# Gates, retention gate, retention queries and keys computed in one Strassen phase that leaves its results in DRAM

## The chip, the cores and the metric

The kernel runs on one core of one Trainium2 chip. The metric is the device time of one execution in microseconds (us). The median of three runs is taken; one further execution is recorded by the profiler.

## What is computed

One decoder block on x of 1024 rows and 1024 channels, all in float32. Cut to what matters here:

```python
xn = rmsnorm(x, norm1_g)
qa, ka, va, qr, kr, vr, gr, gate_a, gate_b = split(xn @ w_in)   # 3x1536, 1024, 1024, 2048, 2048, 1024, 1024 columns
# mixer A: 12 heads of 128 in three groups, dilated windows; the groups of a head slot are
# mixed by their softmax denominators
o_a = combine(attend(rmsnorm(qa), rmsnorm(ka), va))             # 1024 x 512
# mixer B: 4 retention heads, chunks of 128 rows, a state carried from chunk to chunk
o_r = head_groupnorm(retention(qr, kr, vr)) * silu(gr)          # 1024 x 2048
y = sigmoid(gate_a) * (o_a @ w_proj_a) + sigmoid(gate_b) * (o_r @ w_proj_b)
x = x + y @ w_out
x = x + square(relu(rmsnorm(x) @ w_up)) @ w_down
```

## The kernel before

**Arithmetic.** A float32 operand is kept as two tiles of the type fp32r, a rounded part (h) and the rest (l). `split` (L274 to L276) makes them: ScalarE copies h, VectorE subtracts to get l. Each product then takes three matmuls, h·h, h·l and l·h, which `Pipe.group` issues at L186. A *step* (`Pipe.step`, L195) is one such group for one PSUM tile, with small pieces of other work put between its matmuls: `pipe.at(lag, fn)` names a function that is to run inside the step that comes `lag` steps later. So the order on TensorE is written out by hand. The order on the other engines, and on SP's queue, from which every DMA is issued, is chosen by the framework's scheduler before the run, and each of these queues is worked off in that order.

**Weights.** `Weights` (L38) holds six pairs of buffers (wh, wl) of 1024 columns and three raw buffers, with a fourth (`more`) in the Strassen phase. A weight goes by DMA into a raw buffer (L140), and `split` takes it from there into a pair as soon as TensorE has freed that pair (`free`, L165). `add` queues one block; `add_units` (L88) queues a unit of the Strassen product, whose two raw blocks give four pieces, A, B and C of 1024 columns and D of 512, and on which VectorE makes four sums in place (`sums`, L111).

**Strassen.** A unit multiplies 256 weight columns with all 1024 rows and all 1024 channels. Directly that is 8 channel blocks x 4 PSUM tiles x 3 = 96 matmuls of 512 columns. The Strassen form takes 7 products of 4 blocks x 3 = 84 matmuls of 512 columns (`product`, L919, in `strassen_order`, L218). It needs seven tiles of operands: quarters of x and sums of them.

**Stages in order.** The norms and the attention, 12 heads of 8 steps (L410 to L516): each step projects queries, keys and values of one head for 128 rows (24 matmuls of 384 columns), and scores, turning and weighted values of earlier blocks run inside it. Then four retention heads (L564). Each projects its queries (`queries`, 4 steps of 24 matmuls of 512 columns) and its keys (8 steps of 24 matmuls of 256 columns, and `turn_k`, which turns each key block by two transposes). Then come 8 steps that project values, and inside these `decay` (scores of the chunk), `output`, `update` (the state) and `turn_o` run. `combine` (L529), which mixes the three attention groups, runs inside the value steps of the first three heads, for 128 rows at a time; it loads them by one DMA from `acc_d`. Then `gate` (L700) and `project` (L724): the gate projection `gr` for 256 columns, multiplied with the normalised retention output read back from `on_d`, and right behind it that slice's share of `o_r @ w_proj_b`, in groups of six matmuls, added up on VectorE in the SBUF tile `Y`. Then the merge (L781): both sigmoid gates, `o_a @ w_proj_a` (`merge`, L766), and the sum, split again into X. Then `w_out` with the second norm (L873), the up projection in Strassen form (L990) and the down projection (L1004).

Of the kernel before, what the change touches and what calls it, by code (L numbers as in the profile page):

```python
# [25 lines left out]
RH = 4  # L26
# [11 lines left out]
class Weights:  # L38
# [12 lines left out]
    def __init__(self, nc, rawp, wp, split):  # L51
# [6 lines left out]
        self.plain = self.taken = 0  # L58

# [10 lines left out]
    def add(self, src, buf=None):  # L70

        n = self.plain
        buf = n % self.WB if buf is None else buf
# [14 lines left out]
    def add_units(self, srcs):  # L88

        base = len(self.src)  # L90
        self.kept = {}
# [4 lines left out]
        def piece(key, buf, r, cols, then=None):  # L96
            def step():
                if isinstance(buf, tuple):
                    if "D" not in self.kept:
                        self.kept["D"] = self.buffer(buf[0])  # L100
                    h, l = (x[:, 512 * buf[1]:512 * buf[1] + 512] for x in self.kept["D"])
                else:
                    h, l = self.buffer(buf)
# [13 lines left out]
        for j in range(-1, len(srcs)):  # L117
            if j + 1 < len(srcs):
                r = base + 2 * (j + 1)
                piece((j + 1, "A"), self.A[(j + 1) % 2], r + 1, both)  # L120
            if j >= 0:
                r = base + 2 * j
                piece((j, "D"), (self.D, j % 2), r, slice(0, 512), lambda r=r: sums(r))
                piece((j, "B"), self.B[j % 2], r + 1, both, lambda r=r: self.used.add(r + 1))
                piece((j, "C"), self.C, r, both, lambda r=r: self.used.add(r))
# [18 lines left out]
    def pump(self, most=99):  # L144
        while most > 0 and self.next < len(self.steps):
# [3 lines left out]
            while len(self.raw) <= r:  # L149
                assert self.load()  # L150
# [80 lines left out]
def hybrid_block(ctx: ExitStack, tc: tile.TileContext, a: dict, out: bass.AP):  # L231
# [17 lines left out]
    oa_d = dram.tile([SLOTS, P, S], F, name="oa_d")  # L249
    on_d = dram.tile([NF, P, S], F, name="on_d")  # L250
    v_d = dram.tile([HEADS, S, DH], F, name="v_d")
# [39 lines left out]
    src = []  # L291
    for slot in range(SLOTS):
        for g in range(3):
            src += [a["w_att"][g * SLOTS + slot, u] for u in range(4)]
    for h in range(RH):
        src += [a["w_rqk"][h, u] for u in range(4)] + [a["w_rv"][h, u] for u in range(4)]
    src += [a["w_gr"][0, 0], a["w_gr"][0, 1]]
    for j in range(8):
        src += [a["w_pb"][j, 0], a["w_pb"][j, 1]]
        if j < 7:  # L300
            src += [a["w_gr"][j + 1, 0], a["w_gr"][j + 1, 1]]
    for d in range(KT):
        src += [a["w_gate"][d, 0], a["w_gate"][d, 1], a["w_pa"][d]]
    W = Weights(nc, rawp, wp, split)
    for ap in src:
        W.add(ap)
# [4 lines left out]
    W.add_units([a["w_up"][j] for j in range(NU)])  # L311
    for n, ap in enumerate([a["w_down"][c, nb, u] for c in range(8) for nb in range(2) for u in range(2)]):
# [801 lines left out]
```

## Time and profile before

| | |
|---|---|
| median of three runs | 2363.76 us (2363.75 to 2367.91) |
| the profiled execution: its own time | 2367.44 us |
| its span, first to last instruction | 2365.6 us |
| mean granted TensorE clock | 0.998 |
| instructions | 30143 |
| DMA traffic | 236.09 MB |

The page gives the busy time of each engine: PE is TensorE's matmuls, PEld its weight loads, DVE VectorE, ACT ScalarE, POOL GpSimd, and SP the queue that issues the DMAs. Matmuls overlap in their pipeline: a row that says that one took 390 ns does not say that the next began 390 ns later. The chain of work that ended last follows the execution back from its end, at each step to what released it; where it runs along TensorE for a while, its pieces give the true time from matmul to matmul. A view by stretches gives the busy time of each engine between two moments, the number of its instructions, the granted clock, and the share of time and the rate of the DMA engines.

### The profile page before, as it was taken

What the parts mean: (1) busy time and instruction counts of PE and PEld (TensorE: products, weight loads), DVE (VectorE), ACT (ScalarE), POOL (GpSimd) and SP (SyncE); (2) the same over time, 40 slices, a digit from 0 to 9 for tenths busy, and PEclk for the clock granted to TensorE, in tenths of its full rate; (3) what the DMA queues carried; (4) which work ended last, traced back from release to release, by engine and by line L of the source; (5) the groups of instructions that cost most, each with busy time, mean ns of one, the idle gap of its engine ahead of it and who ended that gap; (6) DMA issues with size and microseconds to landing.
All of it is one profiled execution on the core that took longest, in us unless ns stands there. A gap on an engine that the chain in (4) does not pass through costs nothing.

```text
span 2365.6 us, 30143 instructions
## 1 busy us (share of the span) xinstructions
PE 2337.6 (99%) x11704; PEld 2017.1 (85%) x11704; DVE 1112.2 (47%) x2316; ACT 832.0 (35%) x1904; POOL 101.3 (4%) x148
## 2 busy tenths in 40 slices
PE   8999999999999999999999999999899999999999
PEld 7999999998788888878888888888788888788887
DVE  6344443444837353654555542243855555133532
ACT  6444444443424333442211221132566656210010
POOL 1111111110000000000000000000000000000000
PEclk9999999999999999999999999999999999999999
DMA  4212122132321211132222221115244447733601
GB/s 138 81 54 88 57 57 87 52 108 70 106 81 59 71 50 50 54 99 63 78 74 63 72 76 49 45 46 176 90 162 167 160 166 265 286 132 113 248 27 72
DMA packets 118049, 236.09 MB, mean 100 GB/s; under 512 B 8721, under 2 KB 53905, under 8 KB 113810
## 3 DMA queue, kind: packets, MB, share of 16 engines
q1 hardware_dynamic: 117906, 234.17, 30.2%
q8 instruction: 92, 1.51, 0.3%
q14 instruction: 51, 0.42, 0.1%
HBM read 171.12 MB, written 63.01 MB: 99 GB/s over the span
## 4 chain that ended last, share of the span: by engine, by line
PE 92%; DVE 4%; ACT 1%; issue 1%; DMA 1%; POOL 1%; SPq 0%; POOLq 0%; ACTq 0%; DVEq 0%
PE mm L186 68%; PE ms L186 18%; PE ms L451 1%; PE ms L431 1%; PE tr L497 1%; PE ms L444 1%; DVE xl L276 1%; PE tr L673 1%; PE ms L619 0%; DVE St L664 0%; POOL st L649 0%; DVE Sl L276 0%; ACT xh L275 0%; PE tr L598 0%; DVE wl L276 0%
## 5 line engine op out<-in xcount | busy, mean ns | idle before, releaser
L186 PE MATMUL mm<-wh,xh 128*128 128x384 f32 (+2 forms) x1792 | 677.6, 378 | 3.5 <-ACT Yd L1015 3.5
L186 PE MATMUL mm<-wh,xl 128*128 128x384 f32 (+2 forms) x1792 | 632.2, 353 | 2.4 <-DVE xl L276 2.3
L186 PE MATMUL mm<-wl,xh 128*128 128x384 f32 (+2 forms) x1600 | 556.8, 348 | 0.9 <-DVE wl L276 0.9
L276 DVE TENSOR_TENSOR wl<-raw,wh 128x1024 fp32r<-128x1024 f32 (+2 forms) x240 | 265.7, 1116 | 252.9 <-ACT wh L275 251.1
L186 PEld LDWEIGHTS mm<-wh,xh 128*128 128x128 f32 x1792 | 338.9, 189 | 34.4 <-ACT Yd L1015 3.9
L275 ACT ACTIVATE wh<-raw 128x1024 fp32r<-128x1024 f32 (+2 forms) x240 | 231.2, 971 | 388.3 <-PE mm L186 268.0
L186 PEld LDWEIGHTS mm<-wh,xl 128*128 128x128 f32 x1792 | 338.2, 189 | 34.4 <-DVE xl L276 3.7
L186 PE MATMUL mm<-xh,wh 128*128 128x512 f32 x896 | 352.3, 393 | 0.0
L186 PE MATMUL mm<-xl,wh 128*128 128x512 f32 x896 | 349.5, 390 | 1.7 <-DVE xl L276 1.7
L186 PE MATMUL mm<-xh,wl 128*128 128x512 f32 x896 | 349.4, 390 | 0.0
L186 PEld LDWEIGHTS mm<-wl,xh 128*128 128x128 f32 x1600 | 303.7, 190 | 23.2 <-DVE wl L276 1.6
L186 PEld LDWEIGHTS mm<-xl,wh 128*128 128x128 f32 x896 | 168.7, 188 | 36.1 <-DVE xl L276 2.1
L186 PEld LDWEIGHTS mm<-xh,wl 128*128 128x128 f32 x896 | 168.6, 188 | 35.5
L186 PEld LDWEIGHTS mm<-xh,wh 128*128 128x128 f32 x896 | 168.7, 188 | 34.5
L1017 DVE TENSOR_TENSOR Yd<-Yd,mm 128x512 f32<-128x512 f32 x112 | 76.9, 686 | 172.3 <-PE mm L186 171.6
L186 PE MATMUL ms<-oh,wl 128*128 128x512 f32 x256 | 101.1, 395 | 0.0
L186 PE MATMUL ms<-oh,wh 128*128 128x512 f32 x256 | 101.1, 395 | 0.0
L186 PE MATMUL ms<-ol,wh 128*128 128x512 f32 x256 | 101.0, 395 | 0.0
L438 ACT ACTIVATE pr<-s,acc 128x128 f32<-128x128 f32 (+1 forms) x96 | 43.1, 449 | 149.3 <-DVE acc L436 132.2
L733 DVE TENSOR_TENSOR Y<-Y,ms 128x512 f32<-128x512 f32 x112 | 76.1, 685 | 38.1 <-PE ms L186 37.5
L285 POOL TENSOR_TENSOR ssa<-ssa,half 128x2 f32<-128x2 f32 x96 | 66.2, 690 | 423.0 <-DVE ssa L284 418.6
L186 PE MATMUL mm<-wh,h 128*128 128x512 f32 x256 | 79.1, 389 | 0.0
(187 smaller groups left out, 2951.8 us busy)
## 6 DMA issues: line engine op xcount, KB each, us to landing
h_d<-hs SPq DMA_DIRECT2D x64, 512.0 KB, 4.0
raw<-in_w_att SPq DMA_DIRECT2D x48, 384.0 KB, 3.9
raw<-in_w_up SPq DMA_DIRECT2D x32, 512.0 KB, 3.8
raw<-in_w_down SPq DMA_DIRECT2D x32, 512.0 KB, 4.5
xh<-h_d SPq DMA_DIRECT2D x12, 1024.0 KB, 7.2
xl<-h_d SPq DMA_DIRECT2D x12, 1024.0 KB, 8.1
raw<-in_w_rqk SPq DMA_DIRECT2D x16, 512.0 KB, 4.5
raw<-in_w_rv SPq DMA_DIRECT2D x16, 512.0 KB, 3.9
```

Of the source, the lines that this page charges most:

```text
L186: self.nc.tensor.matmul(ps, x, y, start=start, stop=stop, skip_group_check=not first)
L275: nc.scalar.activation(dst_h, src, AF.Copy)
L276: nc.vector.tensor_tensor(dst_l, src, dst_h.bitcast(F), op=OP.subtract)
L285: nc.gpsimd.tensor_tensor(dst, dst, half[:, :w], op=OP.pow)
L431: nc.tensor.matmul(sp[:, :n], qT[:, b * P:(b + 1) * P], kT[:, k0:k0 + n], start=True, stop=True)
L438: nc.scalar.activation(st["p"][:, :n], s[:, :n], AF.Exp, bias=acc[:, b, DH:DH + 1], accum_out=acc[:, b, DH + 1:DH + 2])
L444: nc.tensor.transpose(tp[:, j * P:(j + 1) * P], st["p"][:, j * P:(j + 1) * P], ident)
L451: nc.tensor.matmul(po[:, :DH], st["t"][:, j * P:(j + 1) * P], V[:, k0 // P + j, :], start=(j == 0), stop=(j == nk - 1))
L497: nc.tensor.transpose(pt[:, j, :], qk[:, j, :], ident)
L673: nc.tensor.transpose(pt[:, f, :], it["o"][:, f * P:(f + 1) * P], ident)
L733: nc.vector.tensor_tensor(Y[:, d, cs], Y[:, d, cs], pp, op=OP.add)
L1017: nc.vector.tensor_tensor(Y[:, t, ns], Y[:, t, ns], pm, op=OP.add)
```

## The change

- The order of the heads in the last slot becomes 1, 2, 0, so that the group without dilation comes last. `combine` takes 512 rows of one slot instead of 128 rows of four, with four DMAs instead of one. Six of its eight calls move into the attention steps, two stay in the first retention head.
- Behind the attention a new phase computes, from X, all of gate_a, gate_b, qr, kr and gr. The first three of eight gate pairs are computed directly (12 steps of 24 matmuls), while the memory of the attention comes free and `differences` builds the four further Strassen operands. Then 21 Strassen units run: 5 gate pairs, 8 of queries and keys, 8 of gr. Their results go by DMA to `sg_d` (through a sigmoid), `rqk_d` and `sr_d` (times its sigmoid).
- Retention projects values only. `load_chunk` reads queries and keys of a chunk back, two chunks ahead; `decay` turns the keys by two transposes before it scales them. `load_oa` splits the mixed attention output in the last four chunks.
- Then `o_a @ w_proj_a` runs for all channels, 16 steps of 12 matmuls; each result is multiplied with its gate, read back from `sg_d`, and stored in `pa_d`. Beside these steps `load_o` reads `on_d` and `sr_d`, and makes and splits the operand of the retention projection, 16 row tiles in halves of 512 columns. That projection then runs in two chunks of 8 row tiles, 16 steps of 24 matmuls each: the first leaves its results in `pb_d`, the second adds them, gate and attention part, and splits the sum into X.
- `product` becomes a function for both Strassen phases, with its text otherwise unchanged; the buffers behind a Strassen phase follow the order in which its pieces come free (`cycle`). `Y` is gone.

The core of the diff:

```diff
+    heads = [(slot, g) for slot in range(SLOTS) for g in ((0, 1, 2) if slot < SLOTS - 1 else (1, 2, 0))]
+    W.add_units("in", [a["w_gate_q"][j] for j in range(NG)] + [a["w_rqk_q"][j] for j in range(NQ)]
+                + [a["w_gr_q"][j] for j in range(8)])
...
+    def combine(s, i, p2b):
+        at = p2b.tile([P, 4, 3, DH + 2], F, name="at", bufs=1)
+        rows = acc_d[512 * i:512 * i + 512].rearrange("(t p) (g s) e -> s p t g e", p=P, s=SLOTS)
+        for t in range(4):
+            nc.sync.dma_start(at[:, t], rows[s, :, t])
...
+                if head in (5, 8, 11) and b in (1, 5):
+                    pipe.at(2, combine((head - 5) // 3, b // 5, cmb))
...
+    def gate_out(f, d, cs, src):
+        sg = sgp.tile([P, 512], F, name="sg")
+        nc.scalar.activation(sg, src, AF.Sigmoid)
+        nc.sync.dma_start(sg_d[f, d, :, cs], sg)
...
+                    def differences(k):
+                        x = {}
+                        for j, i in ((0, 0), (0, 1), (1, 1), (1, 0)):
+                            x[j, i] = xp.tile([P, 512], F, name=f"x{j}{i}")
+                            xh, xl = XS[j, i]
+                            nc.vector.tensor_tensor(x[j, i], xh[:, k].bitcast(F), xl[:, k].bitcast(F), op=OP.add)
+                        for name, t, u, op in (("N5", (0, 0), (0, 1), OP.subtract), ("N7", (0, 1), (1, 1), OP.subtract),
+                                               ("N6", (1, 1), (0, 0), OP.add), ("N4", (1, 0), (1, 1), OP.subtract)):
+                            nc.vector.tensor_tensor(x[t], x[t], x[u], op=op)
+                            split(operands[name][0][:, k], operands[name][1][:, k], x[t])
...
+        def result(j, f, cs, src):
+            if j < NG:
+                gate_out(f, 3 + j, cs, src)
+                return
+            n = j - NG
+            sg = src
+            if n >= NQ:
+                sg = sgp.tile([P, 512], F, name="sg")
+                nc.scalar.activation(sg, src, AF.Sigmoid)
+                nc.vector.tensor_tensor(sg, src, sg, op=OP.mult)
+            elif src.space == PSUM:
+                sg = sgp.tile([P, 512], F, name="sg")
+                nc.scalar.activation(sg, src, AF.Copy)
+            nc.sync.dma_start(sr_d[2 * (n - NQ) + f, :, cs] if n >= NQ else rqk_d[n // 2, n % 2, f, :, cs], sg)
+        for j, name in strassen_order(NG + NQ + 8):
+            product("in", j, name, unit, operands, lambda: pu, result)
...
+            qk = [p2.tile([P, 2, P], F, name=x, bufs=3) for x in ("rqT", "rkT")]
+            for i in range(2):
+                nc.sync.dma_start(qk[i], rqk_d[h, i, :, :, ts].rearrange("f p t -> p f t"))
...
                     if c < NT - 1:
+                        pt = tr.tile([P, 4, P], F, name="tr")
+                        for f in range(2):
+                            nc.tensor.transpose(pt[:, f, :], kT[:, f], ident)
...
+                if h == 0 and c in (1, 4):
+                    pipe.at(2, combine(SLOTS - 1, c // 4, p2b))
+                if h == RH - 1 and c >= 4:
+                    load_oa(c - 4)
...
+        pm2 = pool(ph, "pm2", 2)
+        def load_o(places, n):
+            for place in places:
+                for cs in halves():
+                    o, sr = loaded(on_d[n, :, cs], "s1"), loaded(sr_d[n, :, cs], "s2")
+                    nc.scalar.activation(o, o, AF.Identity, scale=gng[:, 0, n:n + 1], bias=gng[:, 1, n:n + 1])
+                    nc.vector.tensor_tensor(o, o, sr, op=OP.mult)
+                    split(place[:, 0, cs], place[:, 1, cs], o)
+                n += 1
+        load_o(oS, 0)
+        for d in range(KT):
+            ua, = W.take(1)
+            uh, ul = W[ua]
+            for cs in halves():
+                sga = loaded(sg_d[0, d, :, cs], "s0")
                 pp = ms.tile([P, 512], F, name="ms")
+                pipe.step(pp, [(uh[:, k * P:(k + 1) * P], ul[:, k * P:(k + 1) * P], oaS[k][0][:, cs], oaS[k][1][:, cs])
+                               for k in range(SLOTS)], {SLOTS - 1: lambda: W.free(ua)} if cs.start else None)
+                nc.vector.tensor_tensor(sga, sga, pp, op=OP.mult)
+                nc.sync.dma_start(pa_d[d, :, cs], sga)
+                if ES is None and not pipe.due:
                     ret.close()
+                    ext = pool(body, "ext", 3, "right")
+                    ES = [slot_of(ext) for _ in range(3)] + [slot_of(pool(e1, "ext1", 1, "right"))]
+                    load_o(as_rows(ES[0]) + as_rows(ES[1]), 4)
+                    load_o(as_rows(ES[2]) + as_rows(ES[3]), 12)
+        load_o(places, 8)
...
         for d in range(KT):
+            ub, = W.take(1)
+            for cs in halves():
+                pp = project(0, d, cs, ub)
+                t = pm2.tile([P, 512], F, name="s0")
+                nc.scalar.activation(t, pp, AF.Copy)
+                nc.sync.dma_start(pb_d[d, :, cs], t)
...
+        for n, (d, cs) in enumerate(work):
+            if n + 1 < len(work):
+                ahead.append(fetch(n + 1))
+            y, sgb, pa = ahead[n]
+            pp = project(1, d, cs, ub)
+            nc.vector.tensor_tensor(y, y, pp, op=OP.add)
+            nc.vector.tensor_tensor(y, y, sgb, op=OP.mult)
+            nc.vector.tensor_tensor(y, y, pa, op=OP.add)
+            split(*X(d, cs), y)
```

`as_rows` views the two tiles of an operand slot as two places of 2 x 1024 columns (h and l); `fetch(n)` loads `pb_d`, `sg_d` and `pa_d` of one step; `project(c, d, cs, ub)` is one step of 24 matmuls over the eight places of chunk c.

More of the change, by code (lines that the diff above doesn't have):

```diff
@@ L408, in hybrid_block @@
         nc.sync.dma_start(dist, a["c_dist"])
-        for head in range(HEADS):
-            slot, g = divmod(head, 3)
+        for head, (slot, g) in enumerate(heads):
             h = g * SLOTS + slot
@@ new lines, in hybrid_block @@
+        ahead = [fetch(0)]
+        for n, (d, cs) in enumerate(work):
+            if cs.start == 0:
+                ub, = W.take(1)
+            if n + 1 < len(work):
[6 more added lines that the diff above has]
+            split(*X(d, cs), y)
+        e1.close()
@@ L1073, in r @@
         return np.arange(lo, lo + n)
+    gates = [np.concatenate([r(GA + d * P, P), r(GB + d * P, P)]) for d in range(KT)]
     a = {
```

498 lines of the change are left out of this document (225 added, 273 removed).

## The prediction

> **What bounds the kernel now.** I read the page first, part 1 and then part 4, the chain of work that ended last.
>
> ```profile
> PE 2337.6 (99%) x11704; PEld 2017.1 (85%) x11704; DVE 1112.2 (47%) x2316; ACT 832.0 (35%) x1904; POOL 101.3 (4%) x148
> PE 92%; DVE 4%; ACT 1%; issue 1%; DMA 1%; POOL 1%; SPq 0%; POOLq 0%; ACTq 0%; DVEq 0%
> ```
>
> TensorE is busy 99% of the span and 92% of the chain lies on it. So a matmul that disappears is worth its own time, if its stage keeps TensorE fed. How much is that? A page row for a 512-column matmul says about 390 ns, but these overlap. Two pieces of the chain in order of time give the true distance:
>
> ```profile
> 1048.99 11.19 PE ms L186 x48
> 1060.18 10.89 PE mm L186 x48
> ```
>
> 10.89 / 48 = 0.2269 us in a projection of long groups; 11.19 / 48 = 0.233 us in `project`, with its groups of six. Last, the view by stretches: the attention; the last retention head whole; its value steps alone; gate, project and merge together; the restart in the second norm; the up projection, which is already in Strassen form; and the 10 us with the densest DMA in packets of 2 KB.
>
> ```profile
> core 0: us, PE busy (x) PEld busy (x) DVE busy (x) ACT busy (x) POOL busy (x), PEclk, DMA share, GB/s
> 10.50:517.80 507.30, 504.47 (x3102) 492.70 (x3101) 221.66 (x720) 233.62 (x904) 69.86 (x102) 1.00 0.24 73
> 902.60:1027.00 124.40, 124.40 (x678) 107.44 (x677) 58.66 (x125) 44.66 (x81) 6.43 (x8) 1.00 0.19 55
> 949.20:1027.00 77.80, 77.80 (x372) 64.72 (x371) 48.18 (x103) 33.30 (x60) 5.88 (x7) 1.00 0.22 68
> 1027.00:1598.00 571.00, 569.34 (x2491) 466.93 (x2490) 257.71 (x362) 131.79 (x187) 0.55 (x1) 1.00 0.21 66
> 1692.80:1715.00 22.20, 15.69 (x66) 12.31 (x67) 19.99 (x33) 11.12 (x18) 0.55 (x1) 0.85 0.19 60
> 1715.00:2010.80 295.80, 295.80 (x1307) 244.91 (x1306) 163.67 (x216) 184.25 (x298) 0.00 (x0) 1.00 0.53 184
> 2000.00:2010.00 10.00, 10.00 (x46) 8.27 (x45) 3.28 (x4) 5.27 (x8) 0.00 (x0) 1.00 1.01 336
> ```
>
> Everywhere around the change TensorE is busy all the time, and no other engine is over two thirds full.
>
> **The gross gain, from matmul counts.** Queries and keys: a head takes 124.40 us, its value steps 77.80, so 46.60 us go into them, 186.4 us for four heads. In Strassen form they are 8 units x 84 matmuls x 0.2269 = 152.5 us. The keys must still be turned, now inside `decay`: 4 heads x 7 chunks x 2 = 56 transposes. Four transposes in a row take from 1035.42 to the next matmul at 1035.80, 0.095 us each:
>
> ```profile
> 1035.42 0.63 PE L673 MATMUL tr<-ident,on 128*128 128x128 f32 x4 [1.66 <-DVE on L651]
> 1035.80 0.48 PE L186 MATMUL mm<-xh,wh 128*128 128x512 f32 x1
> ```
>
> That is 5.3 us. Gain: 186.4 - 152.5 - 5.3 = **28.6 us**.
>
> The stretch of 571.0 us holds 768 matmuls of gr, 768 of the retention projection, 768 of the gates and 192 of the attention projection, 2496. After the change they are 8 x 84 = 672, 768 in long groups, 3 x 96 + 5 x 84 = 708, and 192: 2340 x 0.2269 = 531.0 us. Gain: **40.0 us**, of which 156 matmuls make 35.4; the rest is the shorter distance in long groups and the wait of 1.66 us above, for which I charge anew below. Gross: 68.6 us.
>
> The attention's own work only moves: the last group trails by fewer steps, but every score is still computed. `w_out`, up and down keep their counts.
>
> **Does the Strassen phase keep TensorE fed?** A unit lasts 84 x 0.2269 = 19.06 us. The prices of its work beside TensorE:
>
> ```profile
> L276 DVE TENSOR_TENSOR wl<-raw,wh 128x1024 fp32r<-128x1024 f32 x168 | 203.9, 1223 | 241.0 <-ACT wh L275 239.8
> L275 ACT ACTIVATE wh<-raw 128x1024 fp32r<-128x1024 f32 x168 | 175.7, 1057 | 359.0 <-PE mm L186 259.3 <-PE ms L186 73.2 <-DMA raw<-in_w_up 16.1
> L720 DVE TENSOR_TENSOR sg<-sg,oi 128x512 f32<-128x512 f32 x32 | 22.1, 691 | 0.9
> L717 ACT ACTIVATE sg<-mm 128x512 f32<-128x512 f32 x32 | 19.0, 594 | 129.2 <-PE mm L186 129.1
> ```
>
> VectorE: 3.5 splits x 1.22, four sums, two subtractions and, for gr, four products of 0.69: 11.2 us of 19.06, 59%. ScalarE: 3.5 x 1.06 + 7 x 0.59 = 7.8 us, 41%. The up projection ran beside 55% and 62% with TensorE busy 295.80 of 295.80 us, so I charge nothing here. DMA: about 1 MB in and 1 MB out per 19 us is 110 GB/s, against 184 in the up projection. The cover is thinner only at the start: `differences` costs VectorE 4 x 12 x 0.69 = 33 us, which has to fit between the attention's tail and the first N6. From the fifth of the twelve direct gate steps on, these leave 7 x 24 x 0.2269 = 38 us, and four products of 2.7 us follow before N6: 49 us, against 33 plus some 10 us of weight pieces. I charge 1 us, between 0 and 5.
>
> One price there is new, since sigmoids of the gates and exponentials of the attention's tail now alternate on ScalarE. Before, there was one change of function table within the program:
>
> ```profile
> 1029.03 1.28 ACT L717 ACT_TABLE_LOAD   x1
> 1030.40 0.60 ACT L717 ACTIVATE sg<-mm 128x512 f32<-128x512 f32 x1
> ```
>
> From the load to the next activation it took 1.37 us. I count five changes in the first three gate steps, 6.9 us, beside ScalarE's own 233.62 / 96 = 2.4 us per attention step, 7.3 us for three: 14 of 16.3 us, so it fits, and I charge 0, at most 2. [...]
>
> **`combine` in the attention.** VectorE works 221.66 of 507.30 us there, so there is room for six bursts of some 5.5 us. The stall that it can make is that of an engine held by a load. So far, eight calls cost TensorE less than this row, which also holds the 1.66 us at the end of retention:
>
> ```profile
> PE tr L673 <- DVE on L651: 4.6, 6, 1.7
> L535 DVE TENSOR_TENSOR w<-at 128x4 f32<-128x4 f32 x8 | 1.3, 160 | 9.3 <-DMA at<-acc_d 9.3
> ```
>
> VectorE stood 9.3 us in eight calls. With four DMAs and short lags I take 2 us more, between 0 and 12 (six times a burst's 5.5 us less the slack, 2 us a call).
>
> **The tail of retention.** Behind the last `output` came 24-matmul steps; now there are steps of 12, 2.72 us. The chain to `turn_o` took this long:
>
> ```profile
> 1028.42 0.60 ACT L644 ACTIVATE on<-ms 128x512 f32<-128x512 f32 x1 [2.90 <-PE ms L186]
> 1032.87 0.55 DVE L719 TENSOR_SCALAR oi<-oi,gng 128x512 f32<-128x512 f32 x1 [3.13 <-DMA oi<-on_d]
> 1033.33 0.18 DVE L647 BATCH_NORM_AGGREGATE st<-st 128x2 f32<-128x6 f32 x1
> ```
>
> 1028.42 to 1035.42 is 7.0 us, 3.13 of them VectorE standing before a load. Without that it is 3.9 against a cover of 12 matmuls, 2.72: at least 1 us late; with a load of `load_o` in front, 4.3. I take 3.
>
> **The attention projection with `load_o` beside it: the main cost.** TensorE needs 192 x 0.2269 = 43.6 us, with the last output group 45.6. Behind it stands the first step over chunk 0, which needs eight row tiles, 16 halves. The prices:
>
> ```profile
> oi<-on_d SPq DMA_DIRECT2D x32, 256.0 KB, 2.7
> y_d<-xr SPq DMA_DIRECT2D x16, 256.0 KB, 2.1
> xh<-h_d SPq DMA_DIRECT2D x12, 1024.0 KB, 7.2
> h<-h_d SPq DMA_DIRECT2D x8, 1024.0 KB, 12.6
> ```
>
> - A half: load 2.7, then 0.59 + 0.69 + 0.59 + 0.69; 5.3 us, two buffers, so one per 2.6 us: 16 take 42 us.
> - A step's gate: load 2.7, product 0.69, store 2.1, two buffers: 2.75 us per step, against 2.72 on TensorE.
> - VectorE: 32 + 16 operations of 0.69 and some 6 us of weight splits: 39 us.
> - DMA: 14 halves x 0.52 MB, 14 gates and 15 stores x 0.26, 2.1 MB of weights: 17.0 MB. At the 336 GB/s of the full queue above (share 1.01): 51 us.
>
> So four limits lie between 39 and 51 us where TensorE wants 45.6. Nothing is free to catch up, `load_o` of the later tiles competes, and a load that is late holds VectorE for all. A gain is excluded, since TensorE's matmuls remain. Bounds: 0, and 30 (below). The nearest row is the full queue, 51; I add 8 us for queueing: **13 us**.
>
> Afterwards there is cover again: 24 matmuls, 5.45 us, over three loads (0.79 MB, with weights 190 GB/s) and 3.4 us of VectorE.
>
> **Sum.** 68.6 - 1 - 2 - 3 - 13 = 49.6 us. The profiled execution took 2367.44 us (span 2365.6), 3.7 above the median of 2363.76. So 2317.8 against its own time, and **2314 us** against the median.
>
> **Rivals.**
>
> A: the projection is not held up; DMA and VectorE run ahead, as each limit alone nearly allows. Then 68.6 - 6 = 62.6: 2301 us. For it: three of four limits are below TensorE's.
>
> B: the queue is paced by loaded latency. The same 1 MB load takes 7.2 us or 12.6 where DMA is full, 1.75 times. A gate round is then (4.7 + 0.7 + 3.7) / 2 = 4.55 us, 16 make 73 us, and with queueing TensorE loses 30. Short waits also cost clock: the stretch from 1692.80 got 0.85 of it, 3.3 us lost in 22.20, though its longest wait is this:
>
> ```profile
> PE tr L834 <- DVE x L854: 2.9, 1, 2.9
> ```
>
> Total 68.6 - 6 - 30 - 3 = 29.6: 2334 us. [...]
>
> C: the Strassen phase does not deliver, because 21 units with more results than pairs of buffers run 2 us late each: 42 us lost, net 8, 2356 us. Against it: the up projection's 295.80 of 295.80.
>
> D, slower: SP works its queue in order, and in the attention a weight load can wait long.
>
> ```profile
> SPq L140 <- DVE wl L276: 885.4, 142, 34.8
> SPq L531 <- DVE oa L551: 12.7, 4, 8.9
> ```
>
> If the four loads of `combine` stand behind such a wait of up to 34.8 us, VectorE stands with them, and TensorE after two steps, 2 x 5.28 us: over 20 us six times. 49.6 - 120 = -70: 2434 us. It decides from 49.6 / 6 = 8.3 us per call. Against it: so far these loads waited only for their own buffer, 12.7 us in four times.
>
> **Chances.** Forecast 0.53, A 0.20, B 0.15, C 0.05, D 0.07. About 0.2% (4.7 us) can be told from no change. C lies partly within that: 0.03 same, 0.02 faster. Faster 0.90, same 0.03, slower 0.07. The range takes in the forecast with its bounds, A and B: A with the unknown costs at 0 is 2295, B with the end of `combine`'s range at 12 is 2344; C and D, 0.12, are left out. So 2293 to 2344.
>
> **What would show it.** Right: in the Strassen phase 19.1 us per unit and TensorE without gaps; value steps of 79 us per head; between the last value step and the first step over chunk 0 some 58 us, with waits for VectorE and loads and a DMA share near 1. Wrong: waits there under 5 us (A) or over 25 (B); waits of TensorE in the attention behind `combine`'s loads (D); N-products that wait for weights or `differences`; more than ten table loads.

## The result and the profile after

The changed kernel takes 2365.48 us (median of 20 runs, 2362.87 to 2370.16), the kernel before 2365.11 us in the same session: a ratio of 1.0003, with an interval of 0.9996 to 1.001. No change can be measured, although TensorE has 644 of its 11704 matmuls and transposes less to do. The profiled execution took 2367.1 us, its span is 2365.3. Its page, parts 1 and 2:

```profile
PE 2292.8 (97%) x11060; PEld 1961.2 (83%) x11060; DVE 1169.9 (49%) x2372; ACT 926.5 (39%) x2030; POOL 102.0 (4%) x148
...
PE   8999999999999999999999869999899999999999
...
PEclk9999999999999999999999979999999999999999
```

TensorE is busy 45 us less in a span of the same length, and a dip, in TensorE's row and in that of the clock, lies around slices 23 and 24, that is from 1300 to 1420 us. The view by stretches, cut at the first matmul of each stage, has the same columns as before:

```profile
10.50:537.50 527.00, 513.85 (x3140) 499.16 (x3139) 250.37 (x895) 238.76 (x932) 70.17 (x102) 0.99 0.28 84
537.50:611.00 73.50, 72.56 (x339) 58.94 (x338) 48.31 (x92) 34.69 (x65) 0.69 (x1) 1.00 0.27 95
611.00:1014.00 403.00, 400.64 (x1766) 331.06 (x1765) 186.39 (x232) 149.67 (x216) 0.00 (x0) 1.00 0.36 114
1014.00:1332.40 318.40, 313.08 (x1505) 257.19 (x1505) 205.17 (x489) 140.58 (x259) 24.36 (x31) 0.99 0.30 86
1332.40:1429.20 96.80, 61.81 (x211) 47.53 (x210) 51.26 (x78) 42.87 (x61) 0.55 (x1) 0.79 0.82 264
1429.20:1603.20 174.00, 174.00 (x769) 144.10 (x768) 73.19 (x96) 45.70 (x63) 0.00 (x0) 1.00 0.53 170
1603.20:2365.00 761.80, 751.29 (x3329) 620.60 (x3327) 350.43 (x483) 269.40 (x428) 5.52 (x8) 1.00 0.46 159
```

They are the attention, the direct gate steps, the Strassen phase, the value steps, the attention projection, the retention projection, and all that is from `w_out` on. Beside the terms of the forecast (its sum of 49.6 us, from a span of 2365.6, is a span of 2316.0):

| stage | forecast, us | measured, us | difference |
|---|---|---|---|
| attention, to the last matmul of 384 columns | 517.8 + 2 | 536.7 | +16.9 |
| direct gate steps | 75.5 (what the sum leaves) | 74.4 | -1.1 |
| Strassen phase | 21 x 19.06 + 1 | 402.9 | +1.6 |
| value steps | 4 x 79 | 318.3 | +2.3 |
| attention projection, with retention's tail | 45.6 + 13 + 3 | 96.8 | +35.2 |
| retention projection | 768 x 0.2269 | 174.1 | -0.2 |
| from `w_out` to the end | 767.5 | 762.1 | -5.4 |

The differences add up to the missing 49.3 us. Two stages hold it. In the attention projection TensorE stands still for 35.0 us; and it is busy 61.8 us with matmuls that need 45.6 at full clock, 16.2 us more. Most of that is the clock, 0.79 on average: it stood at half for 41.0 us of the stage, and TensorE worked in 28.4 of these. Its matmuls came 0.427 us apart there, against 0.228 at full clock. By the granted share that costs 14.2 us, by the distances 13.2, both estimates. What TensorE waited for, in the whole kernel (engine and line, what released it: us in total, times, longest):

```profile
PE ms L193 <- DVE s L856: 28.4, 5, 8.8
...
PE ms L193 <- ACT smh L287: 3.6, 1, 3.6
...
PE tr L800 <- DVE on L779: 3.1, 1, 3.1
PE ms L549 <- DVE pT L544: 3.1, 4, 1.4
PE mm L193 <- ACT wh L287: 3.1, 2, 2.8
```

The first is the attention projection: L856 is the product of a result with its gate, which frees the PSUM tile. The second is the first retention step, whose mask landed late. The third is the tail of retention. The last two, with parts of others, are the attention. The stretch of the attention projection in the view of waits, all engines:

```profile
ACT s L836 <- DMA s<-on_d: 31.3, 18, 3.4
PE ms L193 <- DVE s L856: 28.4, 5, 8.8
...
DVE s L837 <- ACT s L836: 23.4, 14, 2.8
...
DVE s L856 <- DMA s<-sg_d: 3.8, 4, 1.8
```

ScalarE stands before `load_o`'s loads, VectorE behind ScalarE, TensorE behind VectorE. The gate's own load is hardly waited for, 3.8 us. What holds the gate's product (L856) is its place: in VectorE's fixed order 22 of `load_o`'s products (L837), one for each half, stand before the thirteenth gate's. That one frees the PSUM tile of the sixteenth and last step, since there are three such tiles. The first and the sixteenth of these products:

```profile
1341.45 0.69 DVE L837 TENSOR_TENSOR s<-s,s 128x512 f32<-128x512 f32 x1 [1.38 <-DMA s<-sr_d]
...
1396.41 0.69 DVE L837 TENSOR_TENSOR s<-s,s 128x512 f32<-128x512 f32 x1 [1.15 <-ACT s L836]
```

So the halves come 54.96 / 15 = 3.66 us apart. The first comes 9.1 us into the stage and the twenty-second 88.2 us; right behind it, at 88.8 and 90.2 us, come the products of the twelfth and the thirteenth gate. The DMA of the stage:

```profile
DMA packets 13619, 25.55 MB, mean 264 GB/s; under 512 B 1423, under 2 KB 2447, under 8 KB 13614
...
s<-on_d SPq DMA_DIRECT2D x25, 256.0 KB, 3.6
s<-sr_d SPq DMA_DIRECT2D x25, 256.0 KB, 3.5
raw<-in_w_pb SPq DMA_DIRECT2D x8, 512.0 KB, 5.5
s<-sg_d SPq DMA_DIRECT2D x15, 256.0 KB, 4.0
pa_d<-s SPq DMA_DIRECT2D x13, 256.0 KB, 3.9
```

25 halves are read there, of which the next stage needs 16 at its start, and eight weight blocks, with which it begins one by one.

In the attention, the loss sits at three changes of head. At the first, after head 4, VectorE and then ScalarE (start, duration, and in brackets the idle time before, with what ended it):

```profile
227.24 0.17 DVE L405 TENSOR_TENSOR w<-at 128x4 f32<-128x4 f32 x1 [3.76 <-DMA at<-acc_d]
...
229.71 0.95 DVE L288 TENSOR_TENSOR wl<-raw,wh 128x768 fp32r<-128x768 f32 x1
```

```profile
227.99 0.21 ACT L409 ACTIVATE w<-w 128x12 f32<-128x12 f32 x1 [4.82 <-DVE w L408]
228.11 1.56 ACT L287 ACTIVATE wh<-raw 128x768 fp32r<-128x768 f32 x2
```

```profile
228.99 0.45 PE L193 MATMUL mm<-wh,xh 128*128 128x384 f32 x1 [0.31 <-ACT wh L287]
230.72 0.52 PE L193 MATMUL mm<-wl,xh 128*128 128x384 f32 x1 [1.28 <-DVE wl L288]
```

This is the second call of `combine` for its slot. Its loads were issued at 221.88, as soon as the first call had read its buffer for the last time, and the scheduler put its first operations at the end of the head. There both engines stand in order before its loads, and right behind in both queues wait the weight pieces of the next head, for which TensorE stands. The second change of head goes the same way, with waits of 2.8 and 1.3 us. At the third, after head 10, VectorE stands before these loads too (3.2 and 2.3 us), but TensorE then waits for pieces of the attention itself (`pT` and `pr`), 4.3 us in five waits. After each of the first two the granted clock was half for 3.4 us, and TensorE's matmuls came 0.32 us apart in place of 0.173; the waits before the first were of 0.3 and 1.3 us.

### The profile page after: what moved, and what is told of

Read it like the earlier page. It is cut to its first block, busy times and chain, and to the rows that moved or that the text cites. A ratio compares the mean times of both kernels' runs of the same rounds, so it can differ in the third digit from the quotient of the medians.

```text
span 2365.3 us, 29821 instructions
## 1 busy us (share of the span) xinstructions
PE 2292.8 (97%) x11060; PEld 1961.2 (83%) x11060; DVE 1169.9 (49%) x2372; ACT 926.5 (39%) x2030; POOL 102.0 (4%) x148
## 4 chain that ended last, share of the span: by engine, by line
PE 45%; DVE 2%; DMA 1%; ACT 1%; issue 1%; POOL 0%; SPq 0%; POOLq 0%; ACTq 0%; DVEq 0%
PE mm L193 35%; PE ms L193 9%; DMA s<-on_d 1%; DVE xl L288 0%; ACT xh L287 0%; PE tr L800 0%; PE ms L744 0%; DMA s<-sr_d 0%; DVE xn L988 0%; ACT s L836 0%; DVE s L837 0%; POOL ssq L297 0%; ACT wh L287 0%; ACT mm L981 0%; DMA s<-sg_d 0%
## 5 line engine op out<-in xcount | busy, mean ns | idle before, releaser
L193 PE MATMUL mm<-wh,xh 128*128 128x384 f32 (+1 forms) x1536 | 604.2, 393 | 3.1 <-ACT wh L287 3.1
L193 PE MATMUL mm<-wh,xl 128*128 128x384 f32 (+1 forms) x1536 | 561.2, 365 | 2.0 <-DVE xl L288 1.9
L193 PE MATMUL mm<-wl,xh 128*128 128x384 f32 (+1 forms) x1344 | 485.9, 362 | 2.6 <-DVE wl L288 2.6
L193 PE MATMUL mm<-xh,wl 128*128 128x512 f32 x720 | 281.0, 390 | 0.0
L193 PE MATMUL ms<-xh,wh 128*128 128x512 f32 x604 | 244.2, 404 | 34.2 <-DVE s L856 28.4
L193 PE MATMUL ms<-xl,wh 128*128 128x512 f32 x604 | 240.8, 399 | 0.0
L193 PE MATMUL ms<-xh,wl 128*128 128x512 f32 x604 | 239.9, 397 | 0.0
L193 PEld LDWEIGHTS ms<-xh,wh 128*128 128x128 f32 x604 | 116.9, 194 | 61.8 <-DVE s L856 24.9
L193 PEld LDWEIGHTS ms<-xh,wl 128*128 128x128 f32 x604 | 116.7, 193 | 25.0
L193 PEld LDWEIGHTS ms<-xl,wh 128*128 128x128 f32 x604 | 116.7, 193 | 23.6 <-DVE xl L288 0.3
L536 ACT ACTIVATE pr<-s,acc 128x128 f32<-128x128 f32 (+1 forms) x96 | 43.2, 450 | 148.9 <-DVE acc L534 135.5
```

The source lines that it names most:

```text
L193: self.nc.tensor.matmul(ps, x, y, start=start, stop=stop, skip_group_check=not first)
L536: nc.scalar.activation(st["p"][:, :n], s[:, :n], AF.Exp, bias=acc[:, b, DH:DH + 1], accum_out=acc[:, b, DH + 1:DH + 2])
```

## The experiments

The theories that the runs were to tell apart: **H**, the engines that stand before `combine`'s loads with the next head's weights behind them cost the 17 us. For the attention projection: **B**, its length is its bytes by a rate that the DMAs do not exceed; **Q**, the gate's rounds through two buffers pace it; **L**, the latency of `load_o`'s loads through two buffers paces it. Later, **P** and **W** are about one of these runs. The last column gives what the traces show of this: how many halves of `load_o` come before the thirteenth result of the stage has left its PSUM tile, and how far apart the first sixteen halves come (in e7, e8 and f2, which make no product there, by the halves' splits).

| run | median, us | ratio to before | attention projection, us | in it: MB, GB/s | halves ahead, us apart |
|---|---|---|---|---|---|
| changed kernel | 2365.48 | 1.0003 (0.9996 to 1.001) | 96.8 | 25.6, 264 | 22, 3.7 |
| e1_combine_back | 2350.13 | 0.9937 (0.9922 to 0.9951) | 98.0 | | 22, 3.8 |
| e2_gate_deep | 2364.48 | 1.0 (0.999 to 1.0009) | 92.7 | 24.4, 264 | 21, 3.8 |
| e3_gate_late | 2343.83 | 0.9907 (0.989 to 0.9925) | 67.2 | 17.3, 258 | 15, 3.7 |
| e4_later_tiles_held | 2360.41 | 0.998 (0.9971 to 0.9989) | 88.1 | 23.6, 268 | 18, 3.6 |
| e5_three_buffers | 2374.30 | 1.0038 (1.0025 to 1.0051) | 103.6 | 27.8, 268 | 27, 2.5 |
| e6_half_bytes | 2357.64 | 0.997 (0.9958 to 0.9981) | 83.7 | 20.9, 250 | 20, 3.8 |
| e7_product_in_retention | 2364.50 | 0.9996 (0.9986 to 1.0005) | 80.3 | 19.9, 248 | 24, 1.8 |
| e8_repaired | 2319.68 | 0.9808 (0.9793 to 0.9822) | 58.0 | 16.1, 278 | 24, 1.7 |
| f1_unused_128_bytes | 2379.63 | 1.0063 (1.005 to 1.0076) | 94.0 | | 22, 3.6 |
| f2_repaired_256_bytes | 2308.23 | 0.9762 (0.9749 to 0.9776) | 58.3 | 16.1, 276 | 24, 1.6 |
| f3_three_edits | 2320.53 | 0.9813 (0.98 to 0.9826) | 66.5 | | 14, 3.7 |

### e1_combine_back: all calls of combine in retention

```diff
-                if head in (5, 8, 11) and b in (1, 5):
-                    pipe.at(2, combine((head - 5) // 3, b // 5, cmb))
...
+                if c in (1, 3, 5) and 3 * h + c // 2 < 2 * SLOTS:
+                    pipe.at(2, combine(*divmod(3 * h + c // 2, 2), p2b))
```

> All eight calls of combine run inside the value steps of the first three retention heads, none in the attention; all else as after the change. Theory H (head-of-line): in the attention the attention stage is 19 us longer since combine's first operation on VectorE and its exponential on ScalarE stand before a load, at a change of heads, with the weight splits of the next head behind them; TensorE has 10 us of gaps there and two stretches of 3.4 us at half clock. Then the attention stage falls by 14 to 17 us, retention grows by about 2, total -12 to -16 us. Rival M (moved work): the stage is longer because six times four transposes and more of the attention's trailing blocks now lie in it; then the attention falls by 3 to 5 us, retention grows by as much, total within 2 us.

15.4 us less than the changed kernel. The attention took 518.8 us, 17.9 less, close to the 517.8 of before; the value steps 4.1 more, so there the same calls are cheap but not free. VectorE's first operation of `combine`, in the changed kernel:

```profile
L405 DVE TENSOR_TENSOR w<-at 128x4 f32<-128x4 f32 x8 | 1.3, 166 | 26.8 <-DMA at<-acc_d 26.8
```

and in this run:

```profile
L405 DVE TENSOR_TENSOR w<-at 128x4 f32<-128x4 f32 x8 | 1.3, 159 | 8.2 <-DMA at<-acc_d 8.2
```

H holds: 26.8 us of standing in eight calls, against 9.3 before and 8.2 here. Of the 17.9 us, 10.5 are idle time of TensorE and 3.4 the clock (half of the 6.8 us at half clock, an estimate); the other 4 are work that M also names, and the value steps grew by as much.

### e2_gate_deep: four buffers for the gate

```diff
-            t = pm2.tile([P, 512], F, name=name)
+            t = pm2.tile([P, 512], F, name=name, bufs=4 if name in ('s0',) else 2)
```

Beside it, what is loaded ahead in chunk 2 shares these buffers in place of `s3`.

> The gate of the attention projection is loaded into four buffers instead of two (the last load of the second chunk takes these buffers too, so that the memory is the same). Theory Q (queue): a gate round of load, product and store goes through two buffers, and each DMA in it stands in SP's queue behind those of load_o, which wait for their own buffers; so a step takes 6 us where TensorE needs 2.72. With four buffers two rounds more are under way: the stage falls from 97 us to 65 to 75, total -20 to -30 us. Theory B (bandwidth): the DMA engines are full (25 MB, share 0.83); then deeper buffers give at most what is left of the share, the stage is 85 us or more, total -10 us or less.

1.0 us less in the median; the stage 4.1 us less. Q falls: with the rounds of two buffers gone, 92.7 us remain (65 to 75 by Q, 85 or more by B). The gate's loads were not what VectorE waited for, and its order still has 21 halves before the thirteenth gate.

### e3_gate_late: the gate moves out of the stage

```diff
-                sga = loaded(sg_d[0, d, :, cs], "s0")
+                sga = pm2.tile([P, 512], F, name="s0")
...
-                nc.vector.tensor_tensor(sga, sga, pp, op=OP.mult)
+                nc.scalar.activation(sga, pp, AF.Copy)
...
+            nc.vector.tensor_tensor(pa, pa, sga, op=OP.mult)
```

The attention part is stored without its gate, which is loaded and multiplied in chunk 2, with the loads of `fetch`.

> The attention projection is stored without its gate (ScalarE copies it out of PSUM), and the gate is loaded and multiplied in the second chunk, as a fourth load per step. Nothing in the stage of the attention projection then waits for a load before PSUM comes free. Theory Q: TensorE runs through its 16 steps in about 46 us, and the first chunk waits only for the first 16 halves of load_o, at 3.6 us each some 58 us: stage 58 to 65 us, total -30 to -38 us, if the second chunk hides one load and one product more. Theory B: 4 of 25 MB fewer: stage about 82 us, total -15 us.

21.7 us less; the stage is 29.6 us shorter. Its stretch and its DMA:

```profile
1337.20:1404.40 67.20, 52.87 (x210) 40.57 (x209) 33.48 (x51) 39.33 (x61) 0.55 (x1) 0.92 0.80 258
```

```profile
DMA packets 9114, 17.33 MB, mean 258 GB/s; under 512 B 922, under 2 KB 1946, under 8 KB 9110
...
s<-on_d SPq DMA_DIRECT2D x18, 256.0 KB, 3.5
s<-sr_d SPq DMA_DIRECT2D x18, 256.0 KB, 4.5
```

The stage lies between the forecasts, 58 to 65 by Q and 82 by B. Of the 8.2 MB that went, 16 gates are 4.2; the rest is that a shorter stage also reads fewer halves ahead, 18 in place of 25. In the second chunk the same loads cost nothing: the retention projection took 174.1 us as before. This run takes away the gate's bytes, its wait, and its place in VectorE's order, so it alone does not tell them apart. But the sixteenth half, the last that the next stage needs at its start, comes 64.0 us into the stage here as in the changed kernel: the halves themselves came no faster with fewer bytes, and the stage now ends with them.

### e4_later_tiles_held and e5_three_buffers: what load_o reads ahead

```diff
-                    load_o(as_rows(ES[2]) + as_rows(ES[3]), 12)
...
+        load_o(as_rows(ES[2]) + as_rows(ES[3]), 12, True)
```

In e4 the tiles 12 to 15 are loaded behind the loop, the first of them into a buffer of the gate, so that it cannot go ahead of the last gate.

> The operand tiles of the second chunk are loaded only behind the last gate of the attention projection (their first load takes a gate buffer, the rest queue behind it). In the changed kernel 25 of the 32 halves were loaded in this stage, 16 are needed at its end. Theory Q: fewer DMAs stand before a gate's, but each round still has load_o's of the first chunk in front: stage 70 to 80 us, total -17 to -27 us, and its DMA share falls. Theory B: 9 halves x 0.52 MB of 25 MB fewer: stage 79 us, total -18 us, at the same DMA share. A third theory, that VectorE is what is short in the stage: its work falls by 9 x 1.4 us, stage 84 us.

```diff
-            t = pm2.tile([P, 512], F, name=name)
+            t = pm2.tile([P, 512], F, name=name, bufs=3 if name in ("s1", "s2") else 2)
```

> load_o's two loads get three buffers each instead of two (the last load of the second chunk takes the gate's buffers, so that the memory is the same). Theory B (bytes): in the four kernels so far the stage of the attention projection moved 25.8, 24.4, 23.6 and 17.3 MB at 257 to 268 GB/s; its time is its bytes over that rate. Then three buffers leave the rate at 265 GB/s, and the stage at 92 to 105 us (later tiles only come sooner): total within 4 us. Theory L (latency): each half waits for its two buffers, 3.9 us per half, and the rate follows from that; then a half takes 2.7 us, the rate rises above 320 GB/s, and the stage falls to 70 to 80 us: total -15 to -25 us.

e4 cut the halves that were read to 21 and the stage by 8.7 us, 5.1 us in all, less than any of its three forecasts (70 to 80, 79 and 84 us for the stage). e5, with a third buffer for both operands of `load_o`, made the kernel 8.8 us slower than the changed one:

```profile
1335.90:1439.50 103.60, 61.96 (x210) 46.13 (x209) 57.05 (x87) 47.67 (x69) 0.55 (x1) 0.79 0.85 268
```

```profile
DMA packets 14860, 27.82 MB, mean 268 GB/s; under 512 B 1560, under 2 KB 2584, under 8 KB 14855
...
s<-on_d SPq DMA_DIRECT2D x30, 256.0 KB, 3.8
```

Both forecasts failed: 92 to 105 us for the stage is right for B, but within 4 us for the kernel is not, and L's 70 to 80 us are far off. The first and the sixteenth product of `load_o` show why:

```profile
1344.61 0.69 DVE L837 TENSOR_TENSOR s<-s,s 128x512 f32<-128x512 f32 x1 [1.12 <-DMA s<-sr_d]
...
1382.82 0.69 DVE L837 TENSOR_TENSOR s<-s,s 128x512 f32<-128x512 f32 x1 [0.24 <-ACT s L836]
```

They come 38.21 / 15 = 2.55 us apart, as L said (2.7). A half thus holds its buffers 2 x 3.66 = 7.3 us with two of them and 3 x 2.55 = 7.6 us with three. What L left out is the order: with more buffers the scheduler put more halves before the gates, 17 in place of 7 before the fourth and 27 in place of 22 before the thirteenth. VectorE works them in that order, so TensorE's next gate stands behind tiles that only the second chunk needs, after the sixteen steps of the first.

### e6_half_bytes: half of sr_d

```diff
-                    o, sr = loaded(on_d[n, :, cs], "s1"), loaded(sr_d[n, :, cs], "s2")
+                    o, sr = loaded(on_d[n, :, cs], "s1"), pm2.tile([P, 512], F, name="s2")
+                    nc.sync.dma_start(sr[:, :256], sr_d[n, :, cs.start:cs.start + 256])
```

Both halves of a block are multiplied with its first 256 columns, so the second 256 get wrong values; number and size of the operations stay.

> load_o reads only the first 256 of each 512 columns of the gated projection and uses them twice, so the second half of each block is multiplied with the wrong values; as many DMAs, instructions and buffers as before. Theory B: 25 x 0.13 = 3.3 MB fewer: stage 84 us, total -12 us. Theory L: nothing but a little latency changes: stage 93 us or more, total -4 us at most.

The stage is 13.1 us shorter, the kernel 7.8 us faster (the profiled execution was the fastest of the seven, 2353.6 us). The stage meets B's forecast, 84 us, but not for B's reason. The load took as long with half the bytes (3.5 us with 256 KB in the changed kernel):

```profile
s<-sr_d SPq DMA_DIRECT2D x22, 128.0 KB, 3.6
```

And the halves came no faster, 57.59 / 15 = 3.84 us apart:

```profile
1339.63 0.69 DVE L839 TENSOR_TENSOR s<-s,s 128x512 f32<-128x512 f32 x1 [0.60 <-DMA s<-sr_d]
...
1397.22 0.69 DVE L839 TENSOR_TENSOR s<-s,s 128x512 f32<-128x512 f32 x1 [1.12 <-ACT s L837]
```

The rate fell to 250 GB/s. What changed is the scheduler's order, 20 halves before the thirteenth gate in place of 22, for which two halves' time is 7.7 us of the 13.1.

### e7_product_in_retention: one load in place of two

```diff
+                it = {"r": p2.tile([P, 4, P], F, name="srT", bufs=3)}
+                nc.sync.dma_start(it["r"], sr_d[4 * h:4 * h + 4, :, ts].rearrange("f p t -> p f t"))
...
+                    nc.vector.tensor_tensor(onT, onT, it["r"], op=OP.mult)
...
-                    o, sr = loaded(on_d[n, :, cs], "s1"), loaded(sr_d[n, :, cs], "s2")
...
+                    o = loaded(on_d[n, :, cs], ("s1", "s2")[cs.start > 0])
```

The norm's scale and bias and the product with `sr_d` move into `turn_o`; their small tile `gng` moves to the constants.

> The norm's scale and bias and the product with the gated projection move into turn_o of the retention (four activations and one product per chunk, the gate read back per chunk), so that load_o reads one finished tile and only splits it. Theory B: half of load_o's bytes, 6.5 of 25.8 MB, go: stage about 73 us; retention has 8 MB more over 318 us and stays; total -24 us. Theory L: one load and a chain shorter by 1.3 us per half: 3.1 us per half, stage 78 us, total -19 us. If retention grows by over 5 us, VectorE's in-order queue is the price there.

The stage is 16.5 us shorter (80.3 us; 73 by B, 78 by L), but the kernel is not faster, where -24 or -19 us were expected. A half now has one load, which goes by turns to two tiles of two buffers each; with four buffers the halves came 1.8 us apart. What VectorE waited for at the gates was now their own load, 15.7 us:

```profile
DVE s L858 <- DMA s<-sg_d: 15.7, 7, 5.0
```

Three stages that the edit does not touch grew: the Strassen phase 408.9 us (402.9), the retention projection 176.8 (174.1), the end 767.5 (762.1), 14.1 us together, with no more idle time of TensorE. No theory so far says why; f1 and f2 are about it.

### e8_repaired: four edits together

e1, e3, e7, and the mask of retention loaded ahead of the Strassen phase.

> Four repairs together, the whole computation kept: combine back in the retention heads, the gate applied in the second chunk, the product in retention, and the mask of the retention loaded before the Strassen phase. By the measured parts -15.6 and -22, by theory B 12.6 MB in the stage (48 us instead of 67), and about 4 us at the first retention step: total 2300 to 2310 us. By theory L the stage is at 55 us and the total 2312 us. If a stage that is now fed shows another wait, 2320 us or more.

45.4 us faster than before, but 10 us short of the forecast of 2300 to 2310. TensorE gets its tiles: the projection takes 58.0 us (48 by B, 55 by L), the attention 516.9. The Strassen phase is again long (408.7).

### f1_unused_128_bytes and f2_repaired_256_bytes: the place of the tiles

What e7 and e8 share is a tile of 128 bytes more among the constants, which lie lowest in SBUF. By the addresses of the program, all that is stacked on them moves up by 128 bytes: `wh0` from byte 29408 of each partition to 29536. Tiles on the other side, which are stacked downwards from the top, stay, such as the operand at 212960. In the changed kernel both addresses leave the same remainder by 256, namely 224; with the tile they are 128 apart.

```diff
+    spare = const.tile([P, 32], F, name="spare")
+    nc.vector.memset(spare, 0.0)
```

> The changed kernel with one tile more, of 128 bytes per partition, that nothing reads; it is written once at the start. All tiles on the left side of SBUF, the weights and the quarters of x among them, lie 128 bytes higher by it, those on the right side, the sums of the Strassen form among them, stay. Theory P (the place of the tiles: in the product-in-retention run the distance from matmul to matmul grew from 226.7 to 230.7 ns in every stage that has operands on both sides): the Strassen phase takes 409 us in place of 402.9, the retention projection 176.8 in place of 174.1, the rest 767.5 in place of 762.1, the direct gate steps stay at 74.4; together 2365 + 14 = 2379 us. Rival W (it was the work moved into retention, its DMAs and operations, that made them longer): no stage changes, 2365 us.

```diff
-        gng = const.tile([P, 2, NF], F, name="gng")
-        nc.sync.dma_start(gng, a["ret_gn"])
+        gng = const.tile([P, 4, NF], F, name="gng")
+        nc.sync.dma_start(gng[:, :2], a["ret_gn"])
```

> The repaired kernel, with the two rows of norm weights in a tile of 256 bytes in place of 128, so that the left side lies 256 bytes higher than in the changed kernel. Theory P with a period of 256 bytes: the distance falls back to 226.7 ns, Strassen 403, retention projection 174.1, the rest 762; 2320 - 13 = 2307 us. Theory P without that period, and rival W: 2320 us as before.

P, the place of the tiles, holds for both, and W, the work moved into retention, falls. A tile that nothing reads made the changed kernel 14.2 us slower: Strassen 409.2, retention projection 176.8, the end 766.8. With 256 bytes the repaired kernel fell to 2308.23 us: 403.5, 174.1, 762.3. The view by stretches counts the matmuls. The changed kernel, in the direct gate steps and then in 200 us of the Strassen phase:

```profile
540.00:605.00 65.00, 64.06 (x300) 52.19 (x300) 44.28 (x85) 30.91 (x57) 0.00 (x0) 1.00 0.26 91
```

```profile
650.00:850.00 200.00, 200.00 (x884) 165.68 (x883) 87.71 (x107) 72.43 (x105) 0.00 (x0) 1.00 0.35 111
```

f1_unused_128_bytes in the same stretches:

```profile
540.00:605.00 65.00, 64.05 (x300) 52.00 (x299) 44.24 (x84) 31.15 (x59) 0.00 (x0) 1.00 0.27 95
650.00:850.00 200.00, 200.00 (x868) 162.74 (x867) 85.47 (x103) 71.78 (x103) 0.00 (x0) 1.00 0.34 106
```

TensorE is busy all the time at full clock, and does 868 matmuls in place of 884. The direct gate steps, 300 and 300, are untouched: there weights and x both lie on the side that moved. The Strassen phase has products of both kinds. The first matmuls of the products N6, N5, N1 and N7 of one unit in f1:

```profile
661.04 0.40 PE L193 MATMUL ms<-xh,wh 128*128 128x512 f32 x1
...
663.83 0.40 PE L193 MATMUL mm<-xh,wh 128*128 128x512 f32 x1
...
666.63 0.39 PE L193 MATMUL mm<-xh,wh 128*128 128x512 f32 x1
...
669.37 0.40 PE L193 MATMUL ms<-xh,wh 128*128 128x512 f32 x1
```

The twelve matmuls of N6 and of N5, whose operand lies on the other side, take 2.79 and 2.80 us; those of N1, a quarter of x, 2.74. Over the whole phase I get 232.9 to 233.7 ns from matmul to matmul in N4 to N7 and 227.9 to 228.1 in N1 to N3, against 226.7 to 227.1 in all seven in the changed kernel. The 1.2 ns more in N1 to N3, whose two operands moved together, are unexplained. In these runs what counts is how the address of TensorE's one operand stands to the other's: 128 bytes off costs 2.7 to 3.1%, 256 nothing. Other distances were not tried.

### f3_three_edits: without the product in retention

> The three edits without the one that lengthened the Strassen phase: all combine calls back in retention, the gate of the attention part loaded in chunk 2, the mask loaded early; norm and product stay in load_o. By the single runs: 2365.5 - 15.4 (combine) - 21.6 (gate) - 3 (first value step waits for no mask) = 2325 us, with an attention projection of about 67 us. If the effects do not add, because what load_o gains from the gate is lost to the combine work that no longer stands in the attention, 2332 or more.

2320.53 us, better than the sum of the single runs by 4 to 5 us, with 66.5 us in the projection. Against it f2 shows what the move of the product is worth when the tiles lie well: 12.3 us.

## Why the prediction was wrong, point by point

- **The gross gain was right.** The Strassen phase took 402.9 us against 400.3 at full pace, with 2.4 us of idle time; the value steps 318.3 against 316; the retention projection 174.1 against 174.3. So were the start of the Strassen phase and the tail of retention (3.1 us, charged 3).
- **The table loads were right**, five more than before (these three and two at L536), and TensorE hardly waited behind them: 0.4 and 0.2 us, each ended by a sigmoid.

```profile
L624 ACT ACT_TABLE_LOAD x3 | 3.8, 1283 | 0.1
```

- **The failed step is "The attention projection with `load_o` beside it"**: 13 us charged, 30 as its bound, 96.8 - 45.6 - 3.1 = 48 measured. The sum compared four limits as if they ran side by side, each against TensorE's 45.6 us. What decided is the first two in series, the gates behind the halves. A half was put at 5.3 us, "two buffers, so one per 2.6 us: 16 take 42 us". It took 7.3 us, one per 3.66: its loads 3.5 to 3.6 us in place of 2.7, and operations on two engines that wait for each other. And 22 halves, not 16, stand in VectorE's order before the gate that TensorE's last step needs: 9.1 + 21 x 3.66 = 86 us to the last of them, 88.2 measured. That a late load holds VectorE for all, the prediction had said; its 8 us for queueing were the price.
- **DMA was not the limit that decided.** The prediction took it for the nearest one, at 51 us. 25.55 MB came in place of 17.0, because nothing holds `load_o` back but its own buffers, at 264 GB/s in place of 336. But that rate follows from the waits: SP stood 44.6 us of the stage before buffers that `load_o`'s operations had yet to free, e6 took bytes away and the halves came no faster, e5 gave a buffer and they did. That the rate lay between 248 and 278 GB/s in all these runs is no ceiling: two slices of 2.0 us in the same stage of e7, one behind the other, moved 360 and 344. Why the loads took 3.5 us in place of 2.7 is open.
- **The clock multiplied it.** 13 to 14 of the 51 us are matmuls at half the clock, by the two estimates above. The prediction had seen this and put 3.3 us of it into rival B (of the 6.8 us at half clock in its stretch TensorE worked in 4.1, so 2.0 by the granted share). In this stage the clock stood at half for 41.0 us, with waits of up to 8.8 us; in the attention it stood at half for 3.4 us after waits of 0.3 and 1.3 us. What makes the clock fall is not shown.
- **"`combine` in the attention" was the second failure**: 2 us charged, 12 as its bound, 16.9 measured (17.9 by e1). The mechanism was named, an engine held by a load, but its price came from the value steps, where VectorE stood 9.3 us in eight calls, and its bound from the length of a burst less TensorE's slack. What counted was where the scheduler places the burst, and what stands behind it: at two of the three changes of head the weights of the next head, for which TensorE had no slack.
- **The rivals.** B was the nearest, with the clock and slower loads in it, but it paced the stage by the gate's rounds, which e2 refutes. D, on the slower side, had engines standing before `combine`'s loads, but put the cause on SP's queue and weighed it at 20 us a call. A and C are out.
- **Not foreseen**: from `w_out` on, 5.4 us were won. Before, the beginning of the down projection had this wait, which is gone:

```profile
PE mm L186 <- ACT Yd L1015: 3.5, 1, 3.5
```

  Behind it the granted clock stood at half for 3.4 us, which costs 1.7 us by that share, an estimate; with the wait that is 5.2 of the 5.4 us. That the other layout of the tiles removed it is only argued.

## What to carry to other kernels

Before you move work under an engine that has no slack left, look at the order in which the other engines will do it: count the pieces of less urgent work that the scheduler *can* put before the urgent ones, not those that the next step needs, and multiply them by the pace at which their buffers let them through. Take the urgent work out of that order (e3, 21.7 us less), or hold the prefetch back by a buffer that the two share (e4, 5.1 us less); more buffers alone made it worse (e5, 8.8 us more). A load with little behind it was cheap only at its place in the engines' queues (VectorE stood 8.2 us before `combine`'s loads in e1, 26.8 in the changed kernel): see what stands right behind it, above all at a change of weights. And when a stage that you did not touch changes its pace with TensorE fully busy, compare the addresses of the tiles (f1, 14.2 us).

## What was not expected of the hardware

- The distance from matmul to matmul changed with the place of its two operands: 226.7 ns, or 233 when one side is moved by 128 bytes, and 226.7 again at 256 (f1 and f2: 868 and 885 matmuls in the same 200 us, 884 in the changed kernel). By what the two operands are coupled is not shown.
- A load of 128 KB took as long as one of 256 KB beside the same other traffic, 3.6 us against 3.5 from issue to landing (e6).
- The best version, f2_repaired_256_bytes, takes 2308.23 us, 0.9762 (0.9749 to 0.9776) of the kernel before: below the forecast of 2314. It keeps the whole computation and repairs the three losses, `combine`, the gate and the late mask; 12.3 us of it come from moving the product, which the forecast change did not do.
